# First tile of a hybrid decoder step: the recurrence's local work and the meta state traced ahead of the meta keys and of attention

## The chip, the cores and the metric

The kernel runs on one core of one Trainium2 chip. The metric is the device time of one execution in microseconds, the median of several runs, lower is better. Before the change the runs took 2179.04, 2200.12 and 2199.63 us, so the median is 2199.63 us.

## What is computed

One layer of a decoder, for 512 prompt tokens behind 16 learned meta tokens, and for 8 samples of 4 new tokens each. The reference, cut to what matters here:

```python
h = rmsnorm(x, norm1_g)
proj = h @ w_in                          # 1024 -> 2560 columns
y_rw, state = rwkv7_time_mix(proj[..., :1792], ...)   # recurrence over tokens, 8 heads x 64
q, k, v = split(proj[..., 1792:])        # 8 query heads, 2 key heads x 64, partial rotary
y_at = softmax(q k^T + band mask, sink) v             # window of 128 keys
x = x + concat([y_rw, y_at]) @ w_out
h2 = rmsnorm(x, norm2_g)
s = (h2 @ w_query) . sub_keys            # two top-16 lists per head, 16 experts of 16384 per head, 8 heads
x = x + sum_k gelu(h2 . expert_u[idx_k]) * gate_k * expert_v[idx_k]
```

The recurrence is `S = S * w + (S a) b^T + v k^T`, `y = S r`, from a state of zero ahead of the meta tokens. The meta tokens also give the first 16 keys of attention. All arithmetic is float32, or two float32r parts of it.

## The kernel before, in words

The 512 prompt tokens are four tiles of 128 tokens. The front end handles tile after tile: projection, recurrence, attention, `w_out`, the queries and the choice of experts. Tiles 0 and 3 and the samples fetch their 128 chosen expert rows per token with indirect DMAs ("gathers", L1032, issued by GpSimd) and work on them on VectorE beside other work. Tiles 1 and 2 are done densely behind the front end: all 16384 experts pass through TensorE in 128 blocks.

What the change and the prediction touch:

- `project` (L209 to L224) computes one block of 128 columns of the projection. It loads the weights (L211), splits them into a float32r high part on ScalarE (L213) and a low part on VectorE (L214), and issues 24 matmuls (L218). The result goes to a DRAM scratch `mscr` (L224). The first 256 token columns of all 20 blocks come first, in a stage of their own (L1268 to L1278). `project_rest` (L1307) does the other 314 columns of the same 20 blocks; its matmuls write tiles of the tag `pD`.
- `rwkv_prep` (L282) makes the decays, keys and receptances of one tile. For tile 0 it is traced within the projection stage (L1274). `wkv_local` (L401) then solves the triangular system within the tile by doubling (L480 to L519); its tiles in PSUM are of the tag `pB` (two buffers) for a prompt tile and `pC` (two buffers) for the 16 meta tokens. `local(i)` (L1125) is both, and needs no state. `meta_wkv` (L1282) is the same for the meta tokens, and `meta_state` (L628) makes the state behind them.
- `wkv_chain` (L607) applies the state: two groups of matmuls (L617, L622), then `gn_out` (L578), a chain over VectorE, ScalarE (L588, L592) and GpSimd (L600 to L602) that ends in the left half of `ycat`, the tile's 1024 mixed features.
- `meta_keys` (L1287) makes rotated keys and values of the meta tokens. `attend(0)` (L1133) loads the tile's q, k and v (L1100), rotates them, and calls `attend_prompt` (L765): for each of the two key heads scores (L789), a scaled copy (L791), the mask (L792), softmax (L747 to L763, exponentials in L756), and for each of two pairs of heads a transposition (L801, L802, recorded as L182 and L184), copies (L805, L806) and the product with the values (L813, L816). It uses `pC` as well. It fills the right half of `ycat`.
- `rest(0, pl0)` (L1140) transposes `ycat` (L1145, copies L1144) and calls `mix_and_retrieve` (L905): `w_out` in 8 blocks (loads L892, matmuls L918), the second norm, the queries in 16 blocks (loads L892, matmuls L952), and the top-16 lists (`two_heads`, L970) on VectorE. The weights are in tiles of the tag `wst`, three buffers, which `project_rest` uses too.
- `first_gathers` (L1319) lets the gathers of tile 0 begin: 128 rows of `expert_u`, then 128 of `expert_v`. They need the choice of experts that `rest(0)` makes. `sample_wkv` (L1296) is the same recurrence for the samples.

The order of the calls at L1329 to L1348 is not the order in which instructions stand on the engines. A scheduler reads the whole trace, gives what is traced earlier the higher priority, follows data and the buffers of each tag, and writes one list per engine. Each engine then works through its list in order, and an instruction that waits holds up everything behind it on its engine. A tag's buffers go to the tiles in the order in which these are traced.

Of the kernel before, what the change touches and what calls it, by code (L numbers as in the profile page):

```python
# [113 lines left out]
def hymba_step(ctx, tc, x_prompt, x_sample, cache_k, cache_v, state_wkv, state_shift, meta, norm1_g, w_in, mu, w0,  # L114
# [40 lines left out]
    def gat(shape=(128, D)):  # L155
        return _t(p0, "gat", GAT, shape)

    def px2():
        return _t(p0, "x2", 1, [128, D])

    def ph2():
        return _t(p0, "h2", 1, [128, D])
# [16 lines left out]
    def transpose(out, in_):  # L179
        k = in_.shape[0]  # L180
        if in_.shape[1] == 128 and len(in_.shape) == 2:
            T.transpose(out, in_, ident[:k, :k])  # L182
        else:
            T.matmul(out, in_, ident[:k, :k], start=True, stop=True)  # L184
# [49 lines left out]
    def st(tag, bufs, shape, dt=F32):  # L234
        return _t(er if tag in _EARLY else sb, tag, bufs, shape, dt)
# [24 lines left out]
    def pC():  # L260
        return _t(pp, "pC", 2, [128, 512])
# [345 lines left out]
    def wkv_chain(r, l, ycat):  # L607

        ends = r["ends"]
        S0 = st("S0", 1, [128, 4, 64])  # L610
        V.tensor_tensor(S0, Sst, bc(ends[:, :, 1:2], [128, 4, 64]), OP.mult)
        for hb in range(2):
            pb = 64 * hb
            A.copy(Sbd[pb:pb + 64, :, hb, :], S0[pb:pb + 64])
        pC_ = pC()[:, 0:256].rearrange("p (a b) -> p a b", a=4)
        for blk in range(4):
            T.matmul(pC_[:, blk, :], l["M"][:, blk, :], S0[:, blk, :], start=True, stop=True)  # L617
        V.tensor_tensor(Sst, pC_, l["Sl"], OP.add)
        V.tensor_tensor(Sst, Sst, bc(ends[:, :, 0:1], [128, 4, 64]), OP.mult)
        pY = pC()  # L620
        for blk in range(4):
            T.matmul(pY[:, 128 * blk:128 * blk + 128], l["R2T"][:, blk, :], Sbd[:, blk].rearrange("p a b -> p (a b)"),  # L622
                     start=True, stop=True)
        Y = st("gn", 2, [128, 512])
        V.tensor_tensor(Y, pY, l["Yl"].rearrange("p a b -> p (a b)"), OP.add)
        gn_out(r, Y, ycat)

    def meta_state(r):  # L628
        n = r["n"]
        pm = pC()  # L630
        for blk in range(4):
            for hb in range(2):
                h = 2 * blk + hb
                hc = slice(64 * h, 64 * h + 64)
                o = pm[64 * hb:64 * hb + 64, 64 * blk:64 * blk + 64]
                T.matmul(o, r["Bn"][:n, hc], r["RW"][:n, 0, h, :], start=True, stop=False)
                T.matmul(o, r["Kn"][:n, hc], r["Vn"][:n, hc], start=False, stop=True)
        V.tensor_tensor(Sst, pm[:, 0:256].rearrange("p (a b) -> p a b", a=4), bc(r["ends"][:, :, 0:1], [128, 4, 64]),
                        OP.mult)
# [81 lines left out]
    def qkv_nat(qk, rows, ti):  # L721

        z = st("qkvn", 2, [128, 832])[:rows]
        p = pC()
        p2 = pC()
        for j in range(4):
            transpose(p[:rows, 128 * j:128 * j + 128], qk[:, j, :])
        for j in range(2):
            transpose(p2[:rows, 128 * j:128 * j + 128], qk[:, 4 + j, :])
        A.copy(z[:, 0:512], p[:rows, :])  # L730
        A.copy(z[:, 512:640], p2[:rows, 0:128])
        A.copy(z[:, 704:832], p2[:rows, 128:256])
        x = z[:, 0:640].rearrange("p (h d) -> p h d", d=64)[:, :, 0:16].rearrange("p h (a b) -> p h a b", a=2)
        rp = C("rope")
        co = bc(rp[:rows, ti, 0, :].unsqueeze(1), [rows, 10, 8])
        si = bc(rp[:rows, ti, 1, :].unsqueeze(1), [rows, 10, 8])
        uw = st("rope", 1, [128, 2, 10, 2, 8])[:rows]
        u, w = uw[:, 0], uw[:, 1]
        for a in range(2):
            G.tensor_tensor(u[:, :, a, :], x[:, :, a, :], co, OP.mult)  # L740
            G.tensor_tensor(w[:, :, a, :], x[:, :, a, :], si, OP.mult)
        G.tensor_tensor(x[:, :, 0, :], u[:, :, 0, :], w[:, :, 1, :], OP.subtract)
        G.tensor_tensor(x[:, :, 1, :], u[:, :, 1, :], w[:, :, 0, :], OP.add)
        A.copy(z[:, 640:704], z[:, 512:576])
        return z
# [278 lines left out]
    def experts(h2, ei, gate, nk, acc, fresh):  # L1024

        pre = _t(p0, "pre", 1, [128, 128])

        def rows(w, use):
            held = []
            for k in range(nk):  # L1030
                r = gat()
                G.indirect_dma_start(out=r, out_offset=None, in_=w[0],  # L1032
                                     in_offset=bass.IndirectOffsetOnAxis(ap=ei[:, k:k + 1], axis=0))
                held.append((k, r))
                if len(held) > LAG:
                    use(*held.pop(0))
                yield True
            for x in held:
                use(*x)

        def dot(k, u):
            V.tensor_tensor_reduce(out=u, in0=u, in1=h2, scale=1.0, scalar=0.0, op0=OP.mult, op1=OP.add,
                                   accum_out=pre[:, k:k + 1])
        yield from rows(eu, dot)
        act = _t(p0, "act", 1, [128, 128])
        A.activation(act[:, 0:nk], pre[:, 0:nk], AF.Gelu)
        V.tensor_tensor(act[:, 0:nk], act[:, 0:nk], gate[:, 0:nk], OP.mult)
        acc = acc()

        def add(k, v):  # L1050
            if k == 0 and fresh:
                V.tensor_scalar(acc, v, act[:, 0:1], None, OP.mult)
            else:
                V.scalar_tensor_tensor(acc, v, act[:, k:k + 1], acc, OP.mult, OP.add)
        yield from rows(ev, add)

    def finish(x2, y, rows, dst, gf, kind="F"):

        rms(x2[:rows], y[:rows], rows, gf, kind)
        DM.dma_start(dst, y[:rows])  # L1060

    def final_g(t):
        G.dma_start(t, fin_g.partition_broadcast(128))
        return t

    def sample_experts():

        h2S = ph2()
        for kg in range(4):
            G.dma_start(h2S[32 * kg:32 * kg + 32, :], hscr_s)  # L1070
        box = []

        def mk():
            box.append(px2())
            return box[0]
        yield from experts(h2S, plS[0], plS[1], 32, mk, True)
        xs2 = ph2()
        G.dma_start(xs2[0:32, :], xscr_s)
        for kg in range(4):
            part = box[0]  # L1080
            if kg:
                part = gat()
                G.dma_start(part[0:32, :], box[0][32 * kg:32 * kg + 32, :])
            V.tensor_tensor(xs2[0:32, :], xs2[0:32, :], part[0:32, :], OP.add)
        finish(xs2, gat(), 32, y_s.rearrange("b s d -> (b s) d"), final_g(gat()))
# [12 lines left out]
    def load_qk(c0, n):  # L1098
        qk = st("qk6", 1, [128, 6, 128])[:, :, 0:n]
        DM.dma_start(qk, mscr[14:20, :, c0:c0 + n].rearrange("k p c -> p k c"))  # L1100
        return qk
# [23 lines left out]
    def local(i):  # L1125
        r = preps.pop(i, None) or rwkv_prep(SP - 1 + 128 * i, 128)
        locals_[i] = r, wkv_local(r)
# [5 lines left out]
    def attend(i):  # L1133
        z = zs[i] = qkv_nat(load_qk(SP - 1 + 128 * i, 128), 128, i)
        if i == 3:
            DM.dma_start(kw_p[0, 0].rearrange("w g d -> w (g d)"), z[:, 512:640])
            DM.dma_start(vw_p[0, 0].rearrange("w g d -> w (g d)"), z[:, 704:832])
        attend_prompt(i, z, zs.get(i - 1), ycat(i))
# [143 lines left out]
    def meta_wkv():  # L1282
        r = rwkv_prep(40, 16)
        wkv_local(r)
        meta_state(r)

    def meta_keys():  # L1287
        zM = qkv_nat(load_qk(40, 16), 16, 5)
        DM.dma_start(vms, zM[:, 704:832])
        pk = pC()  # L1290
        for v_ in range(2):
            transpose(pk[:, 64 * v_:64 * v_ + 16], zM[:, 512 + 64 * v_:640 + 64 * v_])
        A.copy(kTA[:, :, 0:16], pk[:, 0:128].rearrange("p (a b) -> p a b", a=2)[:, :, 0:16])
# [29 lines left out]
    def sample_heads():  # L1323
        sc = st("sco0", 2, [128, 4, 128])
        for kg in range(4):
            DM.dma_start(sc[32 * kg:32 * kg + 32], sscr[:, 4 * kg:4 * kg + 4, :])
        two_heads(sc, [x[:, 0:32] for x in plS], front_tile)
        side.append(sample_experts())
    meta_keys()  # L1329
    attend(0)  # L1330
    meta_wkv()
    local(0)
    wkv_chain(*locals_[0], ycat(0))
    project_rest()
    rest(0, pl0)
# [5 lines left out]
    attend(1)  # L1341
    rest(1, dsel[0])
    sample_heads()
    recur(2)
    attend(2)
# [286 lines left out]
```

## Time and profile before

| What | us |
|---|---|
| median of 3 runs (2179.04 to 2200.12) | 2199.63 |
| the profiled execution's own time | 2204.76 |
| its span in the trace | 2203.0 |
| busy in the span: TensorE, VectorE, GpSimd, ScalarE | 1839.1, 1690.4, 1249.2, 867.3 |

The profile is of one execution; times in it count from the start of its span. PE is a matmul on TensorE, PEld its load of weights, DVE VectorE, ACT ScalarE, POOL GpSimd, SPq the queue that issues most DMAs. Nearly all VectorE instructions have the line of a helper, L126, so they are told apart by their tiles.

### The profile page before, as it was taken

How to read it: one execution, taken by the hardware profiler on the slowest of the kernel's cores; microseconds unless marked ns; L12 is line 12 of the kernel's file. 1: busy time of each engine (PE TensorE's matmuls, PEld its weight loads, DVE VectorE, ACT ScalarE, POOL GpSimd, SP SyncE). 2: the span in 40 equal slices, each digit the busy share in tenths (PEclk: the TensorE clock that was granted, in tenths of full speed). 3: DMA queues.
4: the chain of work that ended last, by engine and by line, in shares of the span. 5: the costliest groups of instructions: out<-in, count | busy, mean ns of one | idle time of the engine just before them, and what ended most of it. 6: DMA issues, size and time to landing. Idle time of an engine off the chain costs nothing.

```text
span 2203.0 us, 37197 instructions
## 1 busy us (share of the span) xinstructions
PE 1839.1 (83%) x13915; PEld 1716.0 (78%) x13915; DVE 1690.4 (77%) x3393; ACT 867.3 (39%) x1963; POOL 1249.2 (57%) x963
## 2 busy tenths in 40 slices
PE   5899975585759868996547897899999999999996
PEld 5888974473647747886446787899999999999995
DVE  5543436788788788799989879997778787787887
ACT  6554422211224313323169634334444444444443
POOL 0110103878784676565624546867667776767774
PEclk9999996556755659898778999999999999999998
DMA  7532473687786789996757887799899999999995
GB/s 222 157 101 84 122 191 102 208 288 248 230 273 199 231 273 318 285 317 222 243 163 242 299 313 239 270 326 340 334 330 331 342 326 336 335 325 343 325 330 178
DMA packets 310154, 569.51 MB, mean 259 GB/s; under 512 B 32787, under 2 KB 194565, under 8 KB 309830
## 3 DMA queue, kind: packets, MB, share of 16 engines
q0 software_dynamic: 84048, 305.70, 39.7%
q1 hardware_dynamic: 225926, 261.43, 36.6%
q8 instruction: 110, 1.80, 0.3%
q14 instruction: 70, 0.57, 0.1%
HBM read 543.07 MB, written 24.60 MB: 258 GB/s over the span
## 4 chain that ended last, share of the span: by engine, by line
PE 51%; DVE 22%; DMA 10%; issue 9%; POOL 5%; ACT 3%; SPq 0%; DVEq 0%; POOLq 0%; ACTq 0%
DVE gat L126 5%; PE acc L1478 5%; PE w L1460 5%; PE w L1461 5%; PE w L1463 5%; PE acc L1479 5%; PE acc L1477 5%; PE w L1446 4%; POOL gat L1032 4%; DVE x L126 4%; PE pD L218 3%; DMA gat<-in_expert_v_dram,ei 3%; PE ps L218 2%; DMA wst<-in_w_query_dram 2%; DMA gat<-in_expert_u_dram,ei 2%
## 5 line engine op out<-in xcount | busy, mean ns | idle before, releaser
L126 DVE SCALAR_TENSOR_TENSOR x<-gat,act,x 128x1024 f32<-128x1024 f32 x287 | 427.9, 1491 | 24.7 <-DMA gat<-in_expert_v_dram,ei 23.4
L1032 POOL DMA_INDIRECT gat<-in_expert_u_dram,ei x256 | 343.0, 1340 | 158.8 <-DVE pre L126 75.7
L1032 POOL DMA_INDIRECT gat<-in_expert_v_dram,ei x256 | 294.4, 1150 | 193.6 <-DVE x L126 73.1
L1453 POOL TENSOR_TENSOR vL<-uv,vH 128x1024 fp32r<-128x1024 f32 x128 | 322.5, 2519 | 56.1 <-ACT vH L1452 54.3
L1478 PE MATMUL acc<-aL,vH 128*128 128x256 f32 x1024 | 290.7, 289 | 17.2 <-DVE aL L126 17.1
L1479 PE MATMUL acc<-aH,vL 128*128 128x256 f32 x1024 | 289.3, 287 | 0.0
L1477 PE MATMUL acc<-aH,vH 128*128 128x256 f32 x1024 | 280.5, 295 | 5.3 <-ACT aH L1469 5.3
L1460 PE MATMUL w<-dhH,uH 128*128 128x256 f32 x1024 | 252.5, 284 | 0.2 <-ACT lsc L1548 0.2
L1461 PE MATMUL w<-dhL,uH 128*128 128x256 f32 x1024 | 251.6, 283 | 0.0
L126 DVE CUSTOM_DVE_ANT_0 gat<-gat,h 128x1024 f32<-128x1024 f32 x160 | 213.5, 1343 | 49.6 <-DMA gat<-in_expert_u_dram,ei 47.8
L1478 PEld LDWEIGHTS acc<-aL,vH 128*128 128x128 f32 x1024 | 200.6, 196 | 19.3 <-DVE aL L126 19.3
L126 DVE CUSTOM_DVE_ANT_0 gat<-gat,lx 128x1024 f32<-128x1024 f32 x128 | 214.4, 1686 | 0.0
L1452 ACT CAST vH<-uv 128x1024 fp32r<-128x1024 f32 x128 | 134.6, 1051 | 195.7 <-issue 131.8
L1479 PEld LDWEIGHTS acc<-aH,vL 128*128 128x128 f32 x1024 | 200.6, 196 | 0.0
L1460 PEld LDWEIGHTS w<-dhH,uH 128*128 128x128 f32 x1024 | 196.9, 192 | 0.5 <-ACT lsc L1548 0.4
L1461 PEld LDWEIGHTS w<-dhL,uH 128*128 128x128 f32 x1024 | 196.8, 192 | 0.1
L1477 PEld LDWEIGHTS acc<-aH,vH 128*128 128x128 f32 x1024 | 188.0, 193 | 6.0 <-ACT aH L1469 5.9
L126 DVE TENSOR_TENSOR uL<-w,uH 128x512 fp32r<-128x512 f32 x256 | 167.6, 681 | 3.0 <-ACT uH L1448 3.0
L126 DVE TENSOR_TENSOR w<-w,gl 128x128 f32<-128x128 f32 x128 | 50.5, 395 | 143.3 <-ACT w L1464 143.2
L1463 PE MATMUL w<-dhH,uL 128*128 128x256 f32 x1024 | 151.9, 287 | 2.8 <-DVE uL L126 2.8
L1448 ACT CAST uH<-w 128x512 fp32r<-128x512 f32 x256 | 139.1, 592 | 8.4 <-PE w L1446 3.0
L1446 PE MATMUL w<-ident,uv 128*128 128x128 f32 x1024 | 141.4, 273 | 0.0
(575 smaller groups left out, 4113.8 us busy)
## 6 DMA issues: line engine op xcount, KB each, us to landing
uv<-in_expert_u_dram SPq DMA_DIRECT2D x128, 512.0 KB, 4.5
uv<-in_expert_v_dram SPq DMA_DIRECT2D x128, 512.0 KB, 5.9
wst<-in_w_query_dram SPq DMA_DIRECT2D x48, 512.0 KB, 5.5
wst<-in_w_out_dram SPq DMA_DIRECT2D x24, 512.0 KB, 6.9
wst<-in_w_in_dram SPq DMA_DIRECT2D x20, 512.0 KB, 4.4
h2T<-in_w_in_dram SPq DMA_DIRECT2D x20, 512.0 KB, 4.1
gscr<-uv SPq DMA_DIRECT2D x10, 1024.0 KB, 6.5
gl<-gscr SPq DMA_DIRECT2D x16, 512.0 KB, 7.4
```

Source lines behind the costliest of these rows:

```text
L126: r = getattr(nc.vector, name)(*args, **kw)
L1032: G.indirect_dma_start(out=r, out_offset=None, in_=w[0], in_offset=bass.IndirectOffsetOnAxis(ap=ei[:, k:k + 1], axis=0))
L1446: T.transpose(p[:, q, :], un[:, 128 * k:128 * k + 128], ident)
L1448: A.copy(uH[:, ks, :], p)
L1452: A.copy(vH, vn)
L1453: G.tensor_tensor(vL, vn, vH.bitcast(F32), OP.subtract)
L1460: T.matmul(pre, uH[:, k, :], hH[:, k, :], start=(k == 0), stop=False)
L1461: T.matmul(pre, uH[:, k, :], hL[:, k, :], start=False, stop=False)
L1463: T.matmul(pre, uL[:, k, :], hH[:, k, :], start=False, stop=(k == 7))
L1477: T.matmul(o, vH[:, ds_], aH, start=(j == 0 and d % 2 == 0), stop=False, skip_group_check=True)
L1478: T.matmul(o, vH[:, ds_], aL, start=False, stop=False, skip_group_check=True)
L1479: T.matmul(o, vL[:, ds_], aH, start=False, stop=(j == 127), skip_group_check=True)
```

## The change

The calls of tile 0 are traced in another order: `local(0)` and `meta_wkv()` now stand first, `meta_keys()` and `attend(0)` behind them. No instruction is added to what is computed, and no other line differs.

```diff
+    local(0)
+    meta_wkv()
     meta_keys()
     attend(0)
-    meta_wkv()
-    local(0)
     wkv_chain(*locals_[0], ycat(0))
     project_rest()
     rest(0, pl0)
```

What the scheduler makes of it, at three places. First TensorE, where the projection stage ends. `pQ` is the last product of the preparation of the meta tokens, `qk` holds the meta tokens' q, k and v, and `AR`, `bt` and `kt` are the prepared tile 0, whose first local products are L433 and L434. Before:

```order
L338 MATMUL pQ_1425<-mpa_1423,cst 128x64
L184 MATMUL pC_1219<-ident,qk_215_1216 16x128 x4
L184 MATMUL pC_1220<-ident,qk_215_1216 16x128 x2
L182 MATMUL pA_966<-ident,AR_944 128x128 x4
L433 MATMUL pB_1673<-AR_944,bt_942 128x256
L434 MATMUL pB_1674<-AR_944,kt_943 128x256
```

With the change:

```order
L338 MATMUL pQ_1628<-mpa_1626,cst 128x64
L182 MATMUL pA_966<-ident,AR_944 128x128 x4
L182 MATMUL pA_972<-ident,bt_942 128x128 x4
L433 MATMUL pB_1220<-AR_944,bt_942 128x256
L434 MATMUL pB_1221<-AR_944,kt_943 128x256
```

The transpositions of the meta tokens' q, k and v are gone from here; the first local products stand where they stood, behind the same preparation.

Second TensorE, where the last block of `project_rest` ends (`pD_2765`). `ax_1214` is `ycat`, and L918 is the first block of `w_out`. Before:

```order
L218 MATMUL pD_2765<-x_6_85,wst_2763 128x314
L218 MATMUL pD_2765<-gat_84,wst_2764 128x314
L182 MATMUL pC_2798<-ident,ax_1214 128x128 x4
L182 MATMUL pC_2804<-ident,ax_1214 128x128 x4
L338 MATMUL pA_3595<-pa_3593,cst 128x160
L918 MATMUL pD_2815<-wst_2813,dx_2797 128x128 x4
```

With the change the last matmul of `project_rest` is followed by the second half of attention's second key head (`L789` are its scores; L368, L433 and L434 belong to the samples):

```order
L218 MATMUL pD_2765<-x_6_85,wst_2763 128x314
L218 MATMUL pD_2765<-gat_84,wst_2764 128x314
L368 MATMUL pA_3613<-rksel,pa_3606 40x8
L789 MATMUL pC_1993<-kTA,qT_1926 128x144 x2
L368 MATMUL pA_3613<-rksel,pa_3606 40x8 x3
L433 MATMUL pB_3657<-ax_3603,bt_3601 40x80
```

and 18 rows further on by the products with the state and only then by `w_out`:

```order
L813 MATMUL pC_2036<-vms,PT_2028 128x64
L816 MATMUL pC_2036<-qkvn_1901,PT_2028 128x64
L617 MATMUL pC_2046<-S_405_2042,M_1569 128x64 x4
L622 MATMUL pC_2053<-Sbd,R2T_1537 128x128 x4
L182 MATMUL pC_2798<-ident,ax_1214 128x128 x4
L182 MATMUL pC_2804<-ident,ax_1214 128x128 x4
L918 MATMUL pD_2815<-wst_2813,dx_2797 128x128 x4
```

Between the two pieces stand the transpositions and products with the values of all four heads of that key head (L184, L182, L813, L816). In the list before, all of attention, L617 and L622 stand ahead of `project_rest`'s last 90 matmuls.

Third VectorE, where the third tile's `w_out` begins (`dx_6652` is that tile, `x_538` collects tile 0's gathered rows `gat`, of which `gat_8806` is the last). Before:

```order
L126 TENSOR_TENSOR dx_6652<-dx_6652,pD_6656 128x128
L126 SCALAR_TENSOR_TENSOR x_538_2810<-gat_8776,act_8424,x_538_2810 128x1024
L126 CAST hl_5735<-sel_5723 128x32
L126 MAX_INDEX idxu_5836<-vals_5835,sco_1194_5766 128x8
L126 TENSOR_REDUCE sR_5761<-dsel_15_109 128x2
```

With the change:

```order
L126 SCALAR_TENSOR_TENSOR x_538_2810<-gat_8806,act_8424,x_538_2810 128x1024
L126 MAX_INDEX idxu_5836<-vals_5835,sco_1194_5766 128x8 x2
L126 MAX_INDEX sel_5723<-top_5722,cand_5717 128x8 x2
L126 TENSOR_TENSOR dsel_15_109<-top_5722 128x32
L126 MAX vals_5835<-sco_1194_5766 128x8 x2
L126 TENSOR_TENSOR dx_6652<-dx_6652,pD_6656 128x128
```

Before, 245 of tile 0's 256 rows stand ahead of the first `dx_6652` row and 11 behind it; with the change all 256 stand ahead. The shift begins in the attention of the samples, where ten more rows stand ahead of the same instruction (150 for 140). From the end of the front end on, the lists are the same. ScalarE's list has 57 table loads in place of 52.

## Rows read from the trace of the kernel before

**Rows 1.** Windows view: stretch in us, its length, engines' busy us, clock, DMA.
```profile
core 0: us, PE busy (x) PEld busy (x) DVE busy (x) ACT busy (x) POOL busy (x), PEclk, DMA share, GB/s
104.00:268.00 164.00, 160.27 (x1301) 140.73 (x1302) 66.27 (x132) 79.91 (x183) 17.85 (x25) 0.98 0.33 94
268.00:300.00 32.00, 20.45 (x170) 18.52 (x169) 6.84 (x20) 6.95 (x17) 0.65 (x2) 0.96 0.80 212
300.00:350.00 50.00, 41.25 (x311) 38.92 (x310) 29.01 (x190) 11.29 (x39) 13.81 (x27) 0.88 0.73 211
350.00:384.00 34.00, 18.11 (x99) 12.84 (x98) 19.95 (x95) 8.68 (x25) 7.43 (x11) 0.60 0.10 28
384.00:675.00 291.00, 188.22 (x1236) 155.18 (x1237) 232.97 (x382) 64.67 (x155) 229.35 (x160) 0.59 0.75 250
675.00:1006.00 331.00, 281.89 (x1790) 243.66 (x1790) 277.88 (x574) 99.00 (x249) 204.09 (x195) 0.76 0.83 267
1006.00:1114.00 108.00, 56.14 (x376) 50.06 (x372) 98.96 (x388) 25.50 (x78) 64.69 (x69) 0.75 0.67 214
```

**Rows 2.** Chain that ended last, 100 to 300 us: start, length, what.
```profile
174.29 0.32 PE pC L184 x2
...
175.19 0.26 PE pC L182
...
178.39 0.36 PE pC L813 x2
...
250.33 0.84 PE pC L617 x8
251.17 0.95 PE pC L622 x8
...
263.71 3.81 PE pD L218 x24
...
273.04 8.54 DMA wst<-in_w_out_dram
...
286.17 5.12 DMA wst<-in_w_out_dram
...
291.42 2.04 PE pD L918 x16
```

**Rows 3.** Costliest groups from 104 to 270 us: busy us, mean ns, idle before.
```profile
L756 ACT ACTIVATE ax<-ax,sD 128x144 f32<-128x144 f32 x8 | 3.2, 404 | 1.4 <-DVE sD L126 1.3
L792 POOL TENSOR_TENSOR ax<-ax,dx 128x576 f32<-128x576 f32 x2 | 2.8, 1418 | 34.4 <-ACT ax L791 34.4
L791 ACT ACTIVATE ax<-pC 128x288 f32<-128x288 f32 x4 | 1.5, 405 | 4.7 <-PE pC L789 4.7
L126 DVE TENSOR_REDUCE sD<-ax 128x4 f32<-128x576 f32 x2 | 1.5, 744 | 2.2 <-POOL ax L792 2.2
L805 ACT COPY PT<-pC 16x256 f32<-16x256 f32 x4 | 1.4, 358 | 7.5 <-PE pC L182 7.5
L592 ACT ACT_TABLE_LOAD x1 | 1.3, 1283 | 0.0
```

**Rows 4.** Timeline, VectorE and ScalarE, end of tile 0's mixed features.
```profile
261.89 2.07 DVE L126 TENSOR_TENSOR wst<-h2T,wst 128x1024 fp32r<-128x1024 f32 x1 [0.82 <-ACT wst L213]
...
265.30 0.66 DVE L126 TENSOR_TENSOR ax<-gn,g 128x512 f32<-128x512 f32 x1
...
267.98 1.07 ACT L1144 COPY dx<-pC 128x512 f32<-128x512 f32 x2
```

**Rows 5.** Chain that ended last, 290 to 420 us: queries of tile 0, first gather.
```profile
326.51 2.06 PE pD L952 x16
...
347.63 3.79 PE pD L952 x16
...
384.32 2.08 POOL gat L1032
```

**Rows 6.** Costliest VectorE groups from 384 to 1114 us.
```profile
L126 DVE SCALAR_TENSOR_TENSOR x<-gat,act,x 128x1024 f32<-128x1024 f32 x128 | 177.7, 1388 | 20.4 <-DMA gat<-in_expert_v_dram,ei 19.8 <-DVE x L126 0.3
```

## Prediction, made blind

> **What bounds the kernel now.** I read the windows first, since a change in one stage is worth what that stage's limit says. From 104 to 268 us tile 0's recurrence, its attention and `project_rest` run together; TensorE is busy 160.27 of 164 us at a granted clock of 0.98, the upper of its two levels, while VectorE works 66 and ScalarE 80 us [rows 1]. So this stage lasts as long as TensorE's work in it, and `project_rest` is what fills every gap between the steps of the serial chains. Then the chain of waits: the last matmuls of `project_rest` start at 263.71 and take 3.81 us, so they end at 267.5, and the next links are loads of `w_out` (8.54 and 5.12 us) with matmuls between, the last one ending at 291.42 + 2.04 = 293.5 [rows 2]. The timeline shows the left half of tile 0's mixed features done at 265.30 + 0.66 = 266.0 and their transposed copy at 267.98 + 1.07 = 269.05 [rows 4]: chain and filler end within 2 us of each other, which is as good as the overlap can get. From 268 to 384 us TensorE waits for loads, then for VectorE's top-16 lists, and the first gather is issued at 384.32 [rows 5]. From there to the front end's end at 1114 VectorE is the busiest engine: 233 of 291 us, 278 of 331, then 99 of 108 [rows 1]. Everything behind 1114 begins when the front end is done, and its lists are unchanged.
>
> **The change, part by part.** The order shows that the first local products of tile 0 stand where they stood. They wait for the preparation, not for attention, so the local work doesn't begin earlier. Counted in the lists, 94 matmuls of `project_rest` stood behind the last local product (L572) before, and 86 do now: it doesn't end earlier among the filler either. What truly moves is the meta keys and attention, from the stage's first half to its end, because `pC` now goes to the meta recurrence first. And since `wkv_chain` and attention share `pC`, in the order of the trace, the two products with the state (L617, L622) come behind all of attention. Before, these chains had TensorE's filler beside them; now their last part has none.
>
> *End of the filler, P.* TensorE's work is the same, so P comes earlier by what now stands behind it. For the second key head that is two pairs of heads with transpositions of about 1.2 us (174.29 to 175.45) and four pairs of products of 0.36 us, so 2 x 2.6 us, and 0.84 + 0.95 us for the state; with scores, about 7 us [rows 2]. P = 267.5 - 7 = 260.5. Bounds: 256 if the 3.7 us in which TensorE was idle are won as well [rows 1]; 267.5 if gaps open earlier in the stage, for instance because on SP the load of tile 0's q and k and the store of the meta values now stand among the last third of the weight loads and hold them up.
>
> *The uncovered chain.* From P: scaled copy 0.4, mask on GpSimd 1.4, maximum 0.75, three small operations some 0.5 (my estimate from the maximum's row, most of which is its 576 columns), four exponentials of 0.4: 4.7 us [rows 3]. Two pairs of heads, each 1.2 of transpositions, two copies of 0.36, 1.44 of products: 2 x 3.3 = 6.6 [rows 2, 3]. The state 1.8. `gn_out` from 252.1 (end of L622) to 266.0 took 13.8 us, with a weight split of 2.07 us and others in its way on VectorE [rows 2, 4]; without them 11 to 12, of which I take 12. The transposed copy another 1.6. Sum 26.7; with hand-overs between engines 28. The lower end is 25 (`gn_out` at 11, no hand-overs), the upper end 36: the same with TensorE's 8 us of small pieces at twice their length. The mixed features are ready at 260.5 + 28 = 288.5, in place of 269.05: 19.5 us late. Queued behind TensorE's waiting products are L617, L622, the transpositions and all of `w_out`; VectorE and ScalarE have only the samples' preparation beside it, which had to be done anyway.
>
> *What comes back.* Three blocks of `w_out` are in their buffers by then. Before, 24.4 us passed from the features to the last matmul (269.05 to 293.5), because the buffers came free only with `project_rest`. Now three blocks go at once, 2.04 us each; the first free buffer is refilled from 2 us on, and five blocks remain in two rounds of loads at 5.1 us, or 8.5 where they are crowded [rows 2]. First round: 2 + 5.1 to 11.5, matmuls to 13.6; second: loads from 9.2, done by 17; last matmul at 17 to 22 us, I take 19. So `w_out` ends at 307.5, 14 us later than 293.5. Ends: 256 + 25 + 17 = 298 (+4.5) and 267.5 + 36 + 22 = 325.5 (+32).
>
> *From there to the first gather* nothing is removed. ScalarE has five more table loads at 1.283 us, 6.4 us in all [rows 3]; ScalarE is busy 11 of 50 us here and little more than a fifth of 384 to 675 [rows 1], so the cost lies between 0 and 6.4; I take 2. The Trainium skill says ("ScalarE: Activation LUTs", What ACT_TABLE_LOAD costs) that a switch also drains the engine and comes to about 2.66 us; by that the five would be 13 us, and the sum 11 us above mine if all were on the path. The rows here have only the load.
>
> *From the first gather to 1114.* A late start of the gathers moves all that follows. On VectorE 11 gathered rows (1.388 us each [rows 6], 15 us) move from behind the third tile's `w_out` to before it. If they sit in the way of the front end's chain they cost 15 us there and are missing at the end, where VectorE is full (99 of 108 us): zero. Ends: if they fall into VectorE's idle 53 us of 675 to 1006, the end gains 15; at the cadence of that stretch (331 / 128 = 2.6 us) they cost 28 and give 15 back, 13 lost. I take 0.
>
> *Sum.* +14 + 2 + 0 = +16 us. On the profiled execution's 2204.76 that is 2220.8; that execution is 5.1 us above the median of 2199.63, so on the scale of the median 2216.
>
> **Rivals.** (1) *TensorE's clock.* The stage from 350 to 384, with TensorE busy 18 of 34 us, was granted 0.60 on the mean, the stage before 0.88 [rows 1], and one block of queries took 3.79 us at 347.63, where that stretch begins, in place of 2.06 [rows 5]. The uncovered chain is such a sparse stretch, and `w_out` and the 16 query blocks follow it. If they run at the lower level, 16 x 1.73 = 28 us are added where loads don't hide it, 14 if half is hidden: 2216 + 14 to 28 = 2230 to 2244. For it: the sparse chain of 28 us. Against: the stage of the queries is mostly waits for loads. The Trainium skill ("TensorE: Matmul & The Clock Gate", Part 1: The HAM clock gate) says that the throttled clock is the default and activity lifts it, which speaks for this rival; the stretch at 0.60 agrees.
>
> (2) *It is paid back.* The chain runs at its lower end, the loads at their fastest, and a few of the moved gathers fill idle time: +4.5 to +6 less 5, so about 2200. For it: all of the samples' preparation is now done ahead of `rest(0)`. Against: that wasn't on the chain.
>
> (3) *Faster.* The 11 gathers all fall into idle time (-15) while the start is late by only 4.5: 2199.6 - 10.5 = 2189; it decides at 1114, if the front end's last tile reaches there earlier than before. For it: VectorE has 111 us of idle time from 384 to 1006 and 9 behind. Against: the gathers themselves then start late, and 19.8 us of the idle time behind 675 is their own wait for their rows [rows 6].
>
> **How the numbers follow.** I give the forecast's own case 0.45 (range 2205 to 2228, about a third of it above 1%), rival 1 0.25, rival 2 0.20, rival 3 0.10. A measurement of this kernel can tell about 1%, 22 us, from no change (its own runs differ by 21): slower means above 2221.6, faster below 2177.6. Slower: 0.14 from the forecast's case and 0.23 from rival 1, 0.37. Faster: only rival 3 with more luck than priced, 0.06. The rest, 0.57, is within 1%. The range from 2188 to 2244 takes in rival 3's time and most of rival 1's; it leaves out about 0.1 on either side together with effects of the new order farther on that no row prices.
>
> **What would show it.** Right: the last L218 of `project_rest` near 260 us; behind it some 28 us with TensorE mostly idle; ScalarE's L1144 near 289; the last `w_out` matmul near 307; first gather near 400; the front end's end near 1130, and nothing different behind. Wrong in a step: P above 267 (gaps among the filler); the chain under 20 us; a clock near 0.5 from 290 to 350 (rival 1); the distance from the first gather to the front end's end, 730 us before, changed by more than 13 us. The whole is wrong if the first gather is not later than before.

## The result, and the profile after

The changed kernel takes 2230.12 us (median, 2215.42 to 2237.42), the kernel before beside it 2194.65 us: a ratio of 1.0132, 95% interval 1.0093 to 1.0170. It is slower by 1.3%, some 29 us. Measured once more it was 1.0135 (1.0092 to 1.0177). The bare medians are 35.5 us apart here and 23.2 in the repetition; the 29 us lie between them. Its profiled execution took 2237.42 us, with a span of 2235.7; [rows 1 to 6] are of a span of 2203.0.

The windows of the changed kernel, columns as in [rows 1]:

```profile
core 0: us, PE busy (x) PEld busy (x) DVE busy (x) ACT busy (x) POOL busy (x), PEclk, DMA share, GB/s
104.00:268.00 164.00, 157.33 (x1248) 137.35 (x1248) 58.34 (x115) 75.10 (x167) 11.32 (x23) 0.96 0.32 93
268.00:300.00 32.00, 17.42 (x83) 12.70 (x81) 9.72 (x27) 7.96 (x20) 4.96 (x4) 0.58 0.16 43
300.00:350.00 50.00, 40.64 (x298) 37.82 (x298) 10.70 (x61) 11.27 (x38) 1.30 (x6) 0.86 0.74 196
...
407.00:696.00 289.00, 192.42 (x1236) 157.18 (x1236) 231.68 (x385) 65.05 (x156) 223.46 (x160) 0.57 0.76 252
696.00:1038.00 342.00, 282.92 (x1767) 244.72 (x1765) 280.58 (x601) 103.94 (x257) 205.42 (x192) 0.74 0.81 260
1038.00:1143.00 105.00, 65.42 (x404) 58.68 (x404) 92.27 (x361) 26.46 (x75) 63.19 (x72) 0.74 0.66 208
```

Against [rows 1] the stretch to read is 268 to 300. Before, it held 170 matmuls at a clock of 0.96 and the DMA engines were busy for 0.80 of it: `w_out`. Now it holds 83, at 0.58, and the DMA share is 0.16: nothing that is large runs there. What does run is in the chain that ended last, from 264 us on (start, length, what; it answers to [rows 2]):

```profile
264.82 3.42 PE pD L218 x22
...
269.13 0.42 ACT ax L791
...
269.62 1.41 POOL ax L792
...
272.28 1.28 ACT L756
...
276.55 0.69 PE pC L813 x2
...
283.96 1.71 PE pC L617 x8
285.67 1.83 PE pC L622 x8
...
290.55 1.28 ACT L592
...
297.28 0.70 DVE ax L126
...
298.12 1.94 PE pC L182 x8
300.06 3.61 PE pD L918 x16
...
306.28 6.14 DMA wst<-in_w_out_dram
...
314.61 5.10 DMA wst<-in_w_out_dram
...
319.85 2.04 PE pD L918 x16
```

The projection ends at 268.2, as late as before (267.5). Behind it stands, piece after piece, what the order had put there: softmax of the second key head, its transpositions and products, the products with the state, the group norm, the transposed copy. `w_out` ends at 321.9 in place of 293.4. The gathers and the load of the first dense tile (the front end's end) follow:

```profile
361.86 1.17 POOL L1032 DMA_INDIRECT gat<-in_expert_u_dram,ei  x1 [2.60 <-DVE sco L126]
...
408.90 6.11 POOL L1032 DMA_INDIRECT gat<-in_expert_u_dram,ei  x1 [13.00 <-DVE pre L126]
```

```profile
1143.31 0.82 SPq L1421 DMA_DIRECT2D uv<-hscr  x2
```

Before, the gather at 408.90 stands at 384.32 [rows 5] and the load at 1110.69. What the prediction and all texts here call the first gather is in truth the sixth: five stand ahead of it, from 361.86 with the change and, before, from

```profile
334.38 1.17 POOL L1032 DMA_INDIRECT gat<-in_expert_u_dram,ei  x1 [3.12 <-DVE top L126]
```

The sixth waits for VectorE's work on the rows of these (`pre`). On the means of two profiles of each kernel the real first one is 26.5 us late and the sixth 24.4, so the readings do not hang on which is taken. Behind the front end both kernels take the same: 1092.4 and 1092.3 us.

### The profile page after: what moved, and what is told of

Its sections match the earlier page's. It is cut to its first block, busy times and chain, and to the rows that moved or that the text cites. A ratio compares the mean times of both kernels' runs of the same rounds, so it can differ in the third digit from the quotient of the medians.

```text
span 2235.7 us, 37207 instructions
## 1 busy us (share of the span) xinstructions
PE 1858.2 (83%) x13915; PEld 1729.6 (77%) x13915; DVE 1684.3 (75%) x3393; ACT 873.6 (39%) x1968; POOL 1246.1 (56%) x963
## 4 chain that ended last, share of the span: by engine, by line
PE 50%; DVE 22%; issue 10%; DMA 8%; POOL 6%; ACT 4%; SPq 0%; DVEq 0%; POOLq 0%; ACTq 0%
DVE gat L126 5%; PE w L1460 5%; PE w L1461 5%; PE w L1463 5%; PE acc L1478 5%; PE acc L1479 5%; PE acc L1477 4%; PE w L1446 4%; POOL gat L1032 4%; DVE x L126 3%; PE pD L218 3%; DMA gat<-in_expert_u_dram,ei 2%; PE ps L218 2%; DMA wst<-in_w_query_dram 2%; PE pD L952 2%
## 5 line engine op out<-in xcount | busy, mean ns | idle before, releaser
L126 DVE SCALAR_TENSOR_TENSOR x<-gat,act,x 128x1024 f32<-128x1024 f32 x287 | 423.9, 1477 | 25.0 <-DMA gat<-in_expert_v_dram,ei 23.2
L126 DVE CUSTOM_DVE_ANT_0 gat<-gat,h 128x1024 f32<-128x1024 f32 x160 | 205.5, 1293 | 52.5 <-DMA gat<-in_expert_u_dram,ei 46.3
```

What stands on the lines that cost most here:

```text
L126: r = getattr(nc.vector, name)(*args, **kw)
```

## The experiments

All stage times, from the profiles, in us. "Features" is the end of the second transposed copy (the L1144 copies), "way" the distance from the first gather to the end of the front end. The ratio is that of the run times to the kernel before on the same chip, with its interval.

| kernel | projection ends | features | `w_out` ends | first gather | way | span | ratio |
|---|---|---|---|---|---|---|---|
| before | 267.5 | 269.1 | 293.4 | 384.3 | 726.4 | 2203.0 | 1 |
| before, again (e8) | 271.7 | 273.3 | 298.4 | 388.9 | 723.0 | 2204.0 | |
| changed | 268.2 | 300.7 | 321.9 | 408.9 | 734.4 | 2235.7 | 1.0132 (1.0093 to 1.0170) |
| changed, again (e7) | 270.8 | 303.2 | 323.4 | 413.2 | 718.7 | 2221.7 | 1.0135 (1.0092 to 1.0177) |
| e1 meta ahead | 278.5 | 289.9 | 309.6 | 399.1 | 725.5 | 2214.3 | 1.0102 (1.0058 to 1.0146) |
| e11 the same again | 279.3 | 290.7 | 310.7 | 399.5 | 731.4 | 2222.3 | 1.0102 (1.0051 to 1.0152) |
| e2 local ahead | 274.9 | 293.9 | 313.6 | 404.8 | 728.3 | 2223.1 | 1.0100 (1.0059 to 1.0142) |
| e3 keys ahead | 265.8 | 293.4 | 313.9 | 405.3 | 744.4 | 2241.3 | 1.0169 (1.0127 to 1.0210) |
| e4 own PSUM tag | 292.5 | 285.3 | 313.4 | 402.3 | 726.2 | 2218.7 | 1.0131 (1.0075 to 1.0187) |
| e5 keys, meta, attention, local | 275.1 | 288.1 | 308.0 | 398.3 | 716.3 | 2204.7 | 1.0035 (1.0008 to 1.0061) |
| e6 filler matmuls | 267.6 | 304.9 | 323.8 | 408.9 | 728.5 | 2226.8 | 1.0221 (1.0187 to 1.0256) |
| e9 before, delayed | 268.4 | 304.7 | 325.4 | 414.8 | 725.1 | 2231.8 | 1.0175 (1.0119 to 1.0230) |
| e10 one key head | 269.6 | 283.0 | 303.0 | 391.5 | 718.3 | 2199.3 | 1.0047 (1.0019 to 1.0076) |
| e12 two more blocks | 270.9 | 272.5 | 297.6 | 387.1 | 722.5 | 2198.9 | 1.0005 (0.9983 to 1.0026) |

Two profiles of one kernel differ by 4 to 5 us ahead of the first gather and by up to 16 behind it, so one way alone proves nothing. The theory (A, and in the later runs C) is that the late start of `w_out` makes the whole loss. Rival B puts it on the order of gathers and table loads farther on, rival D on the rest of the change, with the late features mostly made good.

**e1, the meta recurrence alone ahead:**

```diff
-    local(0)
     meta_wkv()
     meta_keys()
     attend(0)
+    local(0)
```

> Only the meta recurrence is moved: it stands first, then the meta keys, attention, and the local work last. In this order all products of tile 0's attention and both products with the state stand ahead of the last 64 matmuls of the projection, as they did before (last 90), while the order farther on is that of the change: all 256 gathered rows ahead of the third tile's first w_out sum, 57 table loads. Theory A (the uncovered chain behind the projection costs the time): mixed features ready within 3 us of the 269.05 of before, last w_out matmul within 4 us of 293.5, ratio to before 0.997 to 1.004. Rival B (the order farther on, with its gathers and table loads, costs it): ratio 1.008 to 1.015 with the features on time.

Neither came as written. The projection ended 11 us later than before, with as many matmuls up to its end, and the features came another 11 us behind that. The chain between 269 and 290 us:

```profile
269.35 1.28 ACT L313
...
276.24 1.28 ACT L327
...
278.20 1.28 ACT L339
...
287.30 1.97 PE pC L182 x8
```

L313, L327 and L339 belong to the preparation of the samples. Their table loads stand in ScalarE's list among the steps of the group norm, and VectorE's steps of the norm behind steps that wait for them. That the products with the state stand ahead of the projection's last matmuls in the list does not yet cover what follows them. The features were not on time, so this run doesn't separate A from B; `w_out` ended 16 us late, and the kernel is some 22 us slower.

**e2, the local work alone ahead:**

```diff
     local(0)
-    meta_wkv()
     meta_keys()
     attend(0)
+    meta_wkv()
```

> Only the local work is moved ahead; the meta recurrence stands last. Attention's four pairs of products stand ahead of the last 287 matmuls of the projection; the meta state is ready 22 matmuls before its end, and the two products with the state stand behind it. 123 gathered rows of each kind's count (of 128 with the change, 117 before) ahead of the third tile, 53 table loads. Theory A: uncovered are the state's products, the group norm and the transposed copy, 1.8 to 3.5 + 10.5 + 2.2 to 3 us, so the features come 14 to 18 us behind the end of the projection (32 with the change), at 281 to 286; w_out ends 10 to 16 us later than before, ratio 1.004 to 1.008. Rival B: the order farther on lies half-way, 1.006 too, but with the features on time. Read from the features' time, then.

19.0 us were uncovered behind the projection, 1 more than expected. But the projection itself ended 7 us later than before, so the features came 8 us and `w_out` 4 us beyond theory A's ranges, and the ratio is beyond its range too (its interval, from 1.0059, reaches into it). The features were late, as A has it and B has not.

**e3, the meta keys ahead:**

```diff
     local(0)
-    meta_wkv()
     meta_keys()
+    meta_wkv()
     attend(0)
```

> The order of the change, but the meta keys stand ahead of the meta recurrence. Their 12 transpositions then fill TensorE's stall at 106 to 112 us again, in which it waits for table loads with the change. Theory on the end of the projection (the 7 us that were not won were lost in this stall and refilled by the meta keys later): the first matmul of the rest of the projection starts near 115.8 as before (118.3 with the change), and the last one ends 3 to 6 us earlier than the 268.2 of the change. Of attention the second key head's products with the values stay uncovered, its scores do not: 26 us uncovered in place of 32, features at 287 to 293, w_out 7 to 12 us earlier than with the change, ratio to before 1.007 to 1.010. If the stall was not the reason, the projection ends at 268 again and the ratio is 1.010 to 1.013.

The first matmul of the rest of the projection started at 115.5, and the last one ended 2.4 us earlier than in the first profile of the change and 5.0 earlier than in the second; 27.6 us were uncovered, and `w_out` ended 8.0 us earlier. Up to there it is near what was expected; the ratio, 1.0169, is not. The way behind the first gather was 744.4 us, 18 more than before, while everything ahead of it was earlier than in the change. All four of its runs lie between 2234 and 2243 us, so this is not one execution. The loss lies behind the first gather. Its cause stays open; the number of gathers that moved is not it, for e3 has 123 of tile 0's 128 accumulated rows ahead of the third tile, fewer than the change (128).

**e4, attention in its own PSUM tag:** the order of the change, with

```diff
-        p = pC()
+        p = pQ()
```

in the meta keys and in tile 0's attention.

> The order of the change, but the meta keys and tile 0's attention write their products to the buffer of the tag pQ, which is free after the preparations, so they no longer wait for the meta recurrence in pC. All of attention then stands ahead of the last 61 matmuls of the projection and the products with the state ahead of the last 155. Theory A: nothing is uncovered behind the projection; features by 269 or before, w_out's end 288 to 294, ratio to before 0.995 to 1.002. If the order of the calls itself (the local work ahead) cost the time in another way than through the shared buffers, the ratio stays above 1.008.

Missed: by its ratio, 1.0131, the second reading came out. The chain came forward in the list, but the projection's end went back to 292.5. In the windows (before, then e4) and in the chain of e4:

```profile
200.00:240.00 40.00, 40.00 (x437) 36.73 (x438) 11.39 (x23) 18.06 (x47) 0.00 (x0) 1.00 0.26 79
```

```profile
200.00:240.00 40.00, 40.00 (x306) 34.38 (x307) 11.62 (x23) 20.19 (x50) 1.42 (x1) 0.87 0.23 70
```

```profile
269.71 5.19 PE pD L218 x22
...
288.77 3.67 PE pD L218 x24
```

40 us that held 437 matmuls before (357 in the change) hold 306, with TensorE never idle but at a clock of 0.87; and 22 matmuls that take 3.42 us in the change take 5.19. Half of the features were transposed at 277 and the rest at 285, but the projection still held TensorE and the weight buffers. From 104 us to the projection's end TensorE was idle for 8.9 us, where it was 3.7 before, did 39 matmuls more (most of them the samples'), and had a clock of 0.91 in place of 0.98. So the chain is covered here, and `w_out` is late all the same, because the projection is. Cover alone does not explain that: the kernel before covers the same work and ends 21 to 25 us earlier. What sets off the lower clock is open.

**e5, keys, meta, attention, local:**

```diff
-    local(0)
+    meta_keys()
     meta_wkv()
-    meta_keys()
     attend(0)
+    local(0)
```

> Meta keys first, then the meta recurrence, attention, and the local work last. The meta keys' transpositions fill TensorE's stall at 106 to 112 us again, and all of attention and the products with the state stand ahead of the last 47 matmuls of the projection; the 911 matmuls up to the projection's last one are as many as before. The order farther on is that of the change (128 gathered rows of either kind ahead of the third tile, 58 table loads). Theory C (a late start of w_out, from the uncovered chain and from the stall with its lower TensorE clock, is all of the loss): granted clock 1.00 from 119 to the projection's end, that end 266 to 270, features 271 to 277, w_out's end 294 to 300, first gather 385 to 391, ratio 1.000 to 1.004. Rival B (the order farther on costs 5 us or more by itself): first gather the same, but ratio 1.004 to 1.009 and the way from the first gather to the end of the front end 730 us or more, in place of 726.

The ratio fits theory C, the stages don't: the projection ended at 275.1, the features came at 288.1, the first gather at 398.3, 12 us behind the mean of the two profiles of before (386.6). The way was 716.3, 8 us less than the mean of before, and gave most of it back. This speaks against rival B: the order of gathers farther on is that of the change (77 accumulated rows ahead of the second tile's `w_out`, 128 ahead of the third's), and in this kernel it cost nothing.

**e6, filler in the uncovered chain:**

```diff
     project_rest()
+    pf = pD()
+    for k in range(120):
+        T.matmul(pf[:, 0:NC + 2 - NA], hB[0][0][:, 0, 0:128], hB[0][0][:, 0, :], start=True, stop=True)
     rest(0, pl0)
```

> The changed order with 120 more matmuls of 128x314, whose products nobody reads, traced between the rest of the projection and w_out: the list has 48, 23, 23, 15 and 11 of them between the pieces of the uncovered chain, 17 us of work at the upper clock. It asks what TensorE's lower clock costs in that chain. Theory of the clock: the granted clock stays at 0.9 to 1.0 from 268 to 300 in place of 0.50 to 0.58, the pieces of the chain take 0.36 in place of 0.69 us, the first w_out block 2.04 in place of 3.61; features 2 to 6 us earlier than the 300.3 of the change (the 48 matmuls ahead of the first transposition give back some 2 us), w_out's end 2 to 6 us earlier, ratio to before 1.009 to 1.013. If the clock costs nothing here: features 1 to 5 us later than 300.3, since the added matmuls stand in the way, and w_out's end with them.

Its chain (L1337 is the filler):

```profile
268.43 6.98 PE pD L1337 x47
...
279.90 0.36 PE pC L813 x2
...
287.29 0.89 PE pC L617 x8
...
290.41 0.89 PE pC L622 x8
...
304.28 3.05 PE pD L918 x16
```

Its windows:

```profile
268.00:294.00 26.00, 26.00 (x184) 23.42 (x183) 5.24 (x15) 4.80 (x16) 1.42 (x1) 1.00 0.18 48
297.00:305.00 8.00, 2.66 (x12) 2.47 (x13) 2.38 (x5) 1.17 (x2) 2.52 (x2) 0.50 0.23 42
```

The granted clock stayed at 1.00 until 294, and the pieces shrank as the theory of the clock says: transpositions, products and state together 6.98 us, against 12.51 in the change. So the lower clock costs 5.5 us of the chain. But TensorE had to get through 17.6 us of filler in between, features came 4 us later, and from 294 the group norm left it idle and the clock fell to 0.5 again. By the features alone the second reading (the clock costs nothing here) would have come out; the lengths of the pieces decide against it. As a remedy it fails. The ratio, 1.0221, is worse than the profile accounts for: the profiled execution took 2228.59 us, the median is 2243.50, and no profile shows where these 15 us lie.

**e7 and e8, both kernels again:**

> The changed kernel once more, for a second profile of it. It asks how much of the 8 us by which the way from the first gather to the end of the front end is longer than before (734.4 against 726.4) belongs to the change, and how much to one execution. Rival B (the order farther on): 734 again. If it is the execution: the first gather within 1 us of 408.9, but the way behind it 724 to 738, moving with the run's own time.

> The kernel before once more, for a second profile of it, with the same question: the first gather within 1 us of 384.3; the way from there to the end of the front end 726 if it belongs to the order, 716 to 732 with the run's own time if it belongs to the execution.

Both first gathers moved by 4 to 5 us, not by under one, so one profile is that far uncertain. The way of the change was 718.7 the second time against 734.4 the first, that of before 723.0 against 726.4. The 8 us are within what two executions of one kernel differ by; on the means 1.9 are left. So for the change rival B has no support. For other orders something behind the first gather does matter (e3, and e1 against e5), and it is not found.

**e9, a pure delay of the kernel before:**

```diff
     wkv_chain(*locals_[0], ycat(0))
+    for k in range(28):
+        idle = st("gn", 2, [128, 512])
+        V.tensor_copy(idle, ycat(0)[:, 0:512])
+        A.copy(ycat(0)[:, 0:512], idle)
     project_rest()
```

> The order of before, with 28 pairs of copies behind the group norm of tile 0 (VectorE to a spare tile, ScalarE back, same values), one after the other, each pair some 1.0 us (0.36 + 0.59 + hand-overs): a pure delay of the mixed features by 28 us, with the stall at 106 to 112 us filled as before and the preparation untouched. Theory C (the late start of w_out alone makes the loss): features at 295 to 300, w_out's end 316 to 322, first gather 405 to 411, ratio 1.009 to 1.015, like the change. Rival D (the late features are mostly made good further on, and the rest of the change, its stall and its order, costs the time): the same features, but ratio under 1.006.

```profile
283.70 0.63 ACT ax L1337
...
284.35 0.44 DVE gn L126
```

A pair took 1.11 us in place of 1.0 and the first ones waited for the samples' preparation, so the features came at 304.7, 33.5 us behind the mean of before, and all that was forecast came out above its range. The first gather is 28.2 us behind the mean of before, the span 28.3, the ratio 1.0175. Of the change itself only one thing is in this kernel, half of the shift farther on (123 accumulated rows ahead of the third tile, for 117 before and 128 with the change; 54 table loads, for 52 and 57). That half costs nothing that can be told: e12 below has 122 rows and 54 loads, at 1.0005. Rival D falls.

**e10, the changed order without the second key head:**

```diff
-        for g in range(2):
+        if i == 0:
+            V.tensor_copy(ycat[:, 768:1024], z[:, 0:256])
+        for g in range(1 if i == 0 else 2):
```

> The changed order, but tile 0's attention computes only the first key head; the other 256 columns of its features are a copy of the rotated queries (so a quarter of tile 0's mixed features is not computed). What stood behind the end of the projection is then ahead of it: the products with the state stand ahead of the last 22 matmuls (L617) and of the last one (L622). The stall at 106 to 112 us and the order farther on stay as in the change (128 rows, 55 loads). Theory C: 16 to 19 us less are uncovered, features at 278 to 284 in place of 300.3, w_out's end 300 to 306, first gather 388 to 396, ratio 1.001 to 1.007. Rival D: ratio 1.010 to 1.014 all the same, since stall and order are still there.

```profile
268.55 0.91 PE pC L622 x8
...
280.45 1.94 PE pC L182 x8
```

With 13.4 us uncovered in place of 32.4, the features came at 283.0, the first gather at 391.5, and the ratio fell to 1.0047, in the middle of theory C's range. The stall at 106 to 112 us and the order farther on are still there.

**e11, e1 again:**

> The first experiment once more (meta recurrence ahead, then meta keys, attention, local work). It and the order with the meta keys first have the same first gather (399.1 and 398.3) and the same counts of rows farther on, yet 1.0102 and 1.0035. If the place of the meta keys makes that difference: 1.008 or more again, and the way from the first gather to the end of the front end 724 or more (725.5 there, 716.3 with the keys first). If single executions make it: a ratio of 1.003 to 1.008 and a way of 716 to 730.

1.0102 again, with a way of 731.4, as the first reading had it. So e1 and e5, alike up to the first gather, seem to differ behind it. Their intervals overlap a little (1.0051 to 1.0152, 1.0008 to 1.0061), and nothing shows by what the place of the meta keys would act there. Left open.

**e12, the path behind the projection shortened in the kernel before:**

```diff
-            wt = weights(w_out, nb)
+            wt = weights(w_out, nb) if nb > 1 or items[0][5] is not pl0 else (
+                st("h2T", 1, [128, 8, 128]) if nb else _t(p0, "h2", 1, [128, 8, 128]))
+            if nb < 2 and items[0][5] is pl0:
+                DM.dma_start(wt, w_out[0][:, nb * 128:(nb + 1) * 128].rearrange("(k p) c -> p k c", p=128))
```

> The order of before, and the first two of tile 0's eight w_out blocks are loaded to the tiles h2T and h2, which the projection leaves free before its end, so that five blocks are loaded ahead in place of three. It uses what the other runs say: what lies between the projection's end and w_out's end is on the path, and before the change 24 us of it (269.05 to 293.5) are waits for loads. Theory C: features at 268 to 274 as before, three blocks left to load in one round behind them, w_out's end 283 to 289 (293.5 and 298.4 in the two profiles of before), first gather 374 to 381, ratio 0.994 to 0.998. If the loads only crowd each other, or the projection's last loads, w_out's end stays at 292 to 298 and the ratio at 0.999 to 1.002.

No change, 1.0005. A new wait took the old one's place (L921 is `w_out` here):

```profile
274.37 1.58 SPq L224
...
276.00 6.38 DMA dx<-in_x_prompt_dram
...
282.74 7.05 PE pD L921 x48
```

The weights were there, but the two product tiles can't come free before the tile of `x` that they are added to has landed. Its load stands on SP's queue behind the store of the projection's last block (L224), which waits for the projection. A version that beats the kernel before was not found.

## Why the prediction was right, and where its size was not

The direction and the mechanism hold: nothing starts earlier, attention and the chain lose their cover, `w_out` and the gathers start late, and behind the front end nothing differs. The size, +16, was too small: +29 by the ratios. The outcome that the forecast held for the likeliest, within 1% (0.57), did not come; slower had 0.37. The time lies just above the forecast's own case (2205 to 2228), at the lower end of rival 1 (2230 to 2244). That it meets rival 1's number is luck: the loss came by the end of the projection and the chain, not by slow queries. Term by term, on the means of the two profiles of each kernel:

- *End of the filler, P.* This is the step that failed, and with it its ground, that "TensorE's work is the same". I had "P = 267.5 - 7 = 260.5"; it is 269.5 (before, 269.6), above the 267 that I gave as the sign of this. My upper bound, 267.5, was near the value by luck, for the reason that I gave it (loads on SP) is not what happened: behind 118 us TensorE is idle for some 0.5 us up to the projection's end. Two things took the 7 us. The first is in TensorE's timeline from 104 to 120, before and after:

```profile
106.61 2.72 PE L184 MATMUL pC<-ident,qk 128*16 128x128 f32 x12 [1.90 <-DMA qk<-mscr]
...
115.76 0.89 PE L218 MATMUL pD<-gat,wst 128*128 128x314 f32 x2
```

```profile
111.72 1.09 PE L182 MATMUL pA<-ident,bt 128*128 128x128 f32 x4 [4.50 <-DVE mpa L126]
...
118.26 0.89 PE L218 MATMUL pD<-gat,wst 128*128 128x314 f32 x2
```

  From 102 to 110 ScalarE does four table loads for the preparation (L313, L326, L339, L327), with only short steps between them, and TensorE waits for what comes behind them. Before, the meta keys' transpositions stood in that wait. I saw in the order that they had left this place and priced only the place that they left for. They now stand in the full stage (217.5 to 222, the 12 records busy for 1.7 us), and the gap grows:

```profile
104.00:118.00 14.00, 10.27 (x47) 7.08 (x48) 7.39 (x16) 9.90 (x20) 5.23 (x9) 0.76 0.42 108
```

```profile
104.00:118.00 14.00, 7.80 (x26) 5.25 (x26) 6.87 (x17) 8.33 (x16) 1.95 (x3) 0.58 0.30 80
```

  (before, then after). TensorE is idle there for 3.7 us before (4.4 in its second profile), and for 6.2 with the change (7.4 in its second); in e3, which puts the transpositions back, for 4.2. So this makes some 2.7 of the 7 us (the 1.7 is not to be added: before, TensorE was busy with the same transpositions for 2.72, in the gap). e3 ends 2.4 and 5.0 us earlier than the change. The lower clock of this stretch is not the change's alone: the second profile of before has 0.55.

  The second, some 4 us, is in the busy time from 104 to the projection's end, which should have fallen by 7 (before, the change, e1):

```profile
104.00:267.60 163.60, 159.87 (x1297) 140.33 (x1298) 66.14 (x131) 79.52 (x182) 17.61 (x25) 0.98 0.33 93
```

```profile
104.00:268.30 164.30, 157.63 (x1250) 137.48 (x1250) 58.34 (x115) 75.12 (x168) 11.32 (x23) 0.96 0.32 92
```

```profile
104.00:278.60 174.60, 166.10 (x1296) 143.66 (x1296) 62.76 (x126) 82.05 (x186) 13.45 (x23) 0.95 0.30 86
```

  With 47 matmuls fewer it fell by 2.2 us (4.2 between the second profiles). In e1 as many matmuls as before keep TensorE busy for 6.2 us more (2.9 more than in the second profile of before, which took 163.17 at a clock of 0.95). So the same work takes longer in another order. The clock is a part of it; the rest, and how much is noise between profiles, stays open.
- *The uncovered chain.* 28 forecast, 32.4 measured (25 to 36 was the range). Softmax 5.9 for 4.7, since its table load (L756, 1.28 us) stands in the chain; the two pairs of heads 9.8 for 6.6 and the state 3.6 for 1.8, both at the lower clock; the group norm 10.5 for 12; the transposed copy 2.7 for 1.6. So rival 1 was right on the place and wrong on the size: the lower clock costs 5.5 us here and 1.6 in the first block of `w_out` (3.61 for 2.04), and not the 14 to 28 that I gave it through the queries. The stretch of the queries, 300 to 350 before, had 0.88; 28 us later, from 328 to 378, it has 0.90 with the change:

```profile
328.00:378.00 50.00, 43.66 (x328) 40.88 (x326) 31.23 (x194) 12.52 (x44) 13.74 (x27) 0.90 0.74 211
```

  The Trainium skill ("TensorE: Matmul & The Clock Gate", Part 1: The HAM clock gate) makes activity what lifts the clock; e6 agrees, with 1.00 while the filler ran and 0.50 once the group norm left TensorE idle.
- *What comes back.* 19 forecast from the features to the end of `w_out`, 21.2 and 20.2 measured: two rounds of loads as priced, and a slow first block.
- *From there to the first gather.* +2 forecast; 87.0 and 89.8 us against 90.9 and 90.5, so nothing was lost. Where a table load is on the chain, the next step follows at once: L756's load ends at 273.56 and the exponentials start at 273.58. The Trainium skill ("ScalarE: Activation LUTs", What ACT_TABLE_LOAD costs) adds a drain of about 1.38 us; no load here shows one (behind 43 of the change's 57 the next step starts within 0.02 us), and the measurement decides.
- *From the first gather to the front end's end.* 0 forecast; 734.4 and 718.7 against 726.4 and 723.0, a mean of +1.9. The 11 moved gathers cost nothing that can be told from the execution. Over the eleven profiles in which `w_out` starts late (the change twice, e1 to e6, e9 to e11) the first gather is 17.6 us late on the mean and the span 18.3 us longer: the late start is passed on one to one, with a scatter of 10 to 20 us (e5 on one side, e3 on the other).

The sum, on the means: `w_out` 322.6 for 295.9, +26.7; -2.3; +1.9; behind the front end -1.1; together +25.2 between the spans. Against the forecast of 307.5 for `w_out`, P makes 9.0 of the 15 us that are missing, the chain 4.4, the tail 1.7. Rival 2 (paid back) and rival 3 (faster) did not come: both needed the chain at its lower end.

## What to carry to other kernels

When a change moves work to another place, price the place that it leaves as well: what stood in another chain's wait cost little there, and the wait can stay when it is gone (TensorE idle for 6.2 us in place of 3.7). Do not take for granted that the work which stays takes as long as before: here 47 matmuls fewer saved 2 to 4 us in place of 7. Where a filler covers serial chains, a chain that ends behind the filler can be paid for nearly whole (in e9 features 33.5 us late made the span 28.3 us longer), and TensorE worked slower in it than in the rows on which the price was made (12.51 us for the pieces that take 6.98 in e6). One profile locates such a loss within some 5 us; a difference that lies far behind it needs a second profile of each kernel before it is given a cause.

## What the runs showed of the hardware that was not expected

TensorE's clock fell to the lower level in stretches in which the profile shows it never idle. In e5, with the transposition and doubling steps of the local work and attention's products between the matmuls of the projection:

```profile
220.00:226.00 6.00, 6.00 (x44) 4.73 (x42) 2.40 (x4) 5.01 (x12) 0.00 (x0) 1.00 0.43 129
226.00:240.00 14.00, 14.00 (x61) 11.41 (x61) 1.89 (x4) 3.55 (x9) 0.00 (x0) 0.54 0.15 44
```

Busy for 14.00 of 14 us, it did 61 matmuls at 0.54. Shorter ones are in e1 to e4, in e11 and in the second profile of the change (0.79 from 149 to 154), though not in its first one, and none in either profile of before between 124 and 268. So the order of the instructions alone does not decide it. They take part in the late ends of the projection in e1, e2, e4 and e5; what sets them off was not found.
